# One VectorE subtraction per head, issued behind the projections' work instead of in front of it

## The chip, the cores and the metric

The kernel runs on one core of a Trainium2 chip. The metric is the device time of one launch in microseconds (us). Before the change three timed runs gave 684.11, 684.16 and 684.79 us; their median is 684.16 us.

## What is computed

One decoder layer over 528 tokens (16 meta tokens and 512 sequence tokens) of width 1024, in float32: sparse attention with 16 heads, then a SwiGLU feed-forward, each followed by a LayerNorm of `alpha * x + sublayer(x)`. A lightweight ReLU indexer scores every key for every query and keeps the 128 best; the attention of a head is then

```python
logits = q @ k.T * scale + bias[t5_bucket(distance)]      # -inf where not kept or not causal
p = softmax(logits)
out[head] = p @ v
h = layer_norm(alpha * h + concat(out) @ w_o)
h = layer_norm(alpha * h + (silu(h @ w_gate) * (h @ w_up)) @ w_down)
```

## The kernel before

**Products in two parts.** Every float32 operand of a matmul is held as a rounded high part and a low part, `lo = x - hi`, and a product is three matmuls: high by high, high by low, low by high (`mm3`, lines 283 to 289, matmuls at L286, L287, L288). ScalarE (ACT) makes the high part (`act_copy`), and VectorE (DVE) or GpSimd (POOL) the low part (`sub`, line 158, recorded as L159). Results of TensorE (PE) come from PSUM in the same two steps, so an evicted PSUM bank is read first by ACT and then by DVE.

**Weights.** They arrive in chunks of 128 x 1024. SyncE (SP) issues the load into one of three raw buffers (L188), ACT makes the high part, and for a chunk that is cut "late" the low part is not issued at once but put on the list `owed` (lines 199 to 201): columns 0 to 639 for DVE (`SHARE` = 640) and 640 to 1023 for POOL. `settle(engine)` issues what the list holds for that engine, `settle()` all of it (lines 205 to 209). `chunk(name)`, which every projection calls when it begins, also calls `settle()` (line 216). `stream()` (lines 610 to 618) cuts the next chunk of the queue `wq, wk, ..., wo` late and asks for the two loads behind it; the raw buffer of a load is free once ACT, DVE and POOL have read the chunk that was there. A chunk is cut about two projections ahead of the one that uses it.

**The loop over heads** (lines 871 to 928) is software-pipelined by hand; the order of the statements is the order of each engine's queue, since the schedule is manual. In its pass h the loop issues

1. on PE the scores of head h (`a{h}S`, L313 and L314) and the first two groups of transposes of head h-1's softmax (`turn(h-1, last, 0)` and `1`, L696);
2. on DVE the five logits instructions (L653), and on ACT the exponentials (`exps`, L661), of which the first two blocks go first; between them the meta part (`mh`, L687) and the two-part copies of the transposed tiles (`pt` and `ptl`, L156 on ACT and L159 on DVE);
3. `normalise(h, ..., (0, 1))`: a reciprocal on DVE (`rec`, L668) and two multiplications on POOL (`lg<-lg,rec`, L670);
4. `settle(nc.vector)` at line 900: the owed low part on DVE, 640 columns, when there is one;
5. the exponentials of the other two blocks, on ACT;
6. `fill(FILL[0])` at line 911: 2.3 units of the generator of projections (`pair`, lines 562 to 589). It gives one step of PE work at a time, and when the eight steps of a projection are through it evicts the PSUM bank: `queries` (q, ACT L156 and DVE L329) or `keys` (ka, ACT L156 and DVE L159), two instructions on each engine. Then it goes to the next projection, whose `chunk` call settles everything that is owed;
7. `turn(h-1, last, 2)` on PE, `normalise(h, ..., (2, 3))` with its own `rec`, `settle()` for POOL's share, and `part(h-1, 2, t2)`: the last two-part copy (`pt` of 256 columns) and `bd`, the block-diagonal meta part (L711), both on DVE;
8. `halved(2)` (the two parts of finished attention rows, `ath` on ACT and `atl` on DVE), `fill(FILL[1])`, and `values(h-1)`: eleven matmuls into `av` (L726), the last of which reads `bd`; ACT then copies half of it (`avt`) and DVE adds (`att`, L735);
9. `stream()`.

After the projections come the output projection, which starts inside the loop (`first_outputs`), LayerNorm, the feed-forward and the second LayerNorm.

PSUM has two banks for projections (`mm`), three for scores, two for transposes (`pt`) and one for `av`. A projection of the keys is done in two halves of 264 columns, each in a bank of its own.

Of the kernel before, what the change touches and what calls it, by code (L numbers as in the profile page):

```python
# [117 lines left out]
def trunk(ctx, tc, a, out):  # L118
    nc = tc.nc
# [38 lines left out]
    def sub(eng, o, x, y):  # L158
        eng.tensor_tensor(out=o, in0=x, in1=y.bitcast(F32), op=ALU.subtract)  # L159
# [45 lines left out]
    def settle(*engs):  # L205

        for x in [x for x in owed if not engs or x[0] in engs]:
            sub(*x)
            owed.remove(x)
# [99 lines left out]
    def scores(q2, ka, kb, name):  # L309
        banks = [bank(f"{name}S{i}", "S") for i in range(3)]  # L310
        for b, i, c, k0, n in REGIONS:
            o = banks[i][:, c : c + n]
            nc.tensor.matmul(o, q2[:, b * P : (b + 1) * P], ka[:, k0 : k0 + n], start=True, stop=False)  # L313
            nc.tensor.matmul(o, q2[:, b * P : (b + 1) * P], kb[:, k0 : k0 + n], start=False, stop=True)  # L314
        return banks
# [287 lines left out]
    def bias_load(h):  # L603
        if h < H:
            tzs[h] = sm.tile([P, 256], F32, name=f"tz{h}", tag="tz", bufs=2)
            nc.sync.dma_start(
                tzs[h], bass.AP(tensor=rbig.tensor, offset=rbig.offset + h * P * 384 + 127, ap=[[383, P], [1, 256]])
            )

    def stream(late=True):  # L610

        group, i = g_qk, where[using[0]][1]
        n = sum(c[0] in split for c in group)
        if n < min(i + 3, where["wo3"][1]):
            cut(group, n, late)
            n += 1
        load(group, n)
        load(group, n + 1)
# [21 lines left out]
    def bias(h, order=(1, 0, 3, 2)):  # L640
        if h < H:
            for b in order:
                n = min(W[b], 256)
                nc.gpsimd.tensor_tensor(  # L644
                    out=bm.at(b, W[b] - n, W[b]), in0=mask.at(b, W[b] - n, W[b]), in1=tzs[h][:, 256 - n :], op=ALU.add
                )

    def logits(h, banks, order):
        lg, mn = Logits(wide(f"lg{h}")), small(f"mn{h}", 5)
        for i in order:  # L650
            b, m, c, k0, n = REGIONS[i]
            init = mn[:, 1:2] if k0 else 3e38
            nc.vector.tensor_tensor_reduce(  # L653
                out=lg.at(b, k0, k0 + n), in0=banks[m][:, c : c + n], in1=bm.at(b, k0, k0 + n),
                scale=1.0, scalar=init, op0=ALU.add, op1=ALU.min, accum_out=mn[:, i : i + 1],
            )
        return lg, mn, small(f"den{h}", 4)

    def exps(lg, mn, den, n):
        b, i = ((1, 0), (0, 2), (3, 3), (2, 4))[n]  # L660
        nc.scalar.activation(  # L661
            lg.blk(b), lg.blk(b), AF.Exp, bias=mn[:, i : i + 1], scale=-1.0, accum_out=den[:, b : b + 1]
        )

    def normalise(h, lg, den, blocks=range(NB)):
        b0, b1 = min(blocks), max(blocks) + 1
        rec = small(f"rec{h}", 4)
        nc.vector.reciprocal(rec[:, b0:b1], den[:, b0:b1])  # L668
        for b in blocks:
            nc.gpsimd.tensor_tensor(  # L670
                out=lg.blk(b), in0=lg.blk(b), in1=rec[:, b : b + 1].to_broadcast([P, W[b]]), op=ALU.mult
            )
# [9 lines left out]
    def meta_parts(h, lg):  # L682

        x = metas[h] = sm.tile([P, P], F32R, name=f"mh{h}", tag="mh", bufs=1)
        xv = x.rearrange("p (r s t j) -> p r s t j", r=2, s=2, t=2)
        act_copy(xv[:, :, :, 0, :], lg.meta())
        nc.vector.tensor_tensor(  # L687
            out=xv[:, :, :, 1, :], in0=lg.meta(), in1=xv[:, :, :, 0, :].bitcast(F32), op=ALU.subtract
        )

    def turn(h, lg, n):

        pieces, cols = PLAN[n]
        pt = bank(f"pt{h}_{n}", "pt")
        for j, b, c in pieces:
            nc.tensor.transpose(pt[:, c : c + P], lg.at(b, NM + j * P, NM + (j + 1) * P), ident)  # L696
        if n == 2:
            nc.tensor.transpose(pt[:, cols : cols + P], metas[h].bitcast(F32), ident)
        return pt

    def part(h, n, pt):

        pieces, cols = PLAN[n]
        hi = unit(f"pt{h}_{n}", F32R)
        lo = hi[:, 256:] if cols == 256 else unit(f"ptl{h}_{n}", F32R)
        act_copy(hi[:, :cols], pt[:, :cols])
        sub(nc.vector, lo[:, :cols], pt[:, :cols], hi[:, :cols])
        parts[h, n] = (hi[:, :cols], lo[:, :cols])
        if n == 2:
            x = unit(f"bd{h}", F32R)[:, :S]  # L710
            nc.vector.tensor_tensor(  # L711
                out=x.rearrange("p (b q) -> p b q", q=P),
                in0=pt[:, cols : cols + P].rearrange("p (o q) -> p o q", o=1).to_broadcast([P, NB, P]),
                in1=diag.rearrange("p (b o) -> p b o", o=1).to_broadcast([P, NB, P]),
                op=ALU.mult,
            )
            parts[h, 3] = (x,)
# [55 lines left out]
    def halved(most=8):  # L773

        n = KT if paired else FEW
        for _ in range(most):
            if len(ath) < min(n, ready[0] // 2):
                halves()
# [61 lines left out]
    def broadcast(names, tiles):  # L840
        for n in names:
            for hf in range(2):
                t = tiles[n, hf] = unit(f"{n}_{hf}", tag="kq")[:, :512]
                nc.sync.dma_start(t, a[n][:, hf * 512 : hf * 512 + 512].to_broadcast([P, 512]))

    def x_load():
        for b in range(NB):
            y.append([unit(f"y{b}{hf}", tag="kq")[:, :512] for hf in range(2)])
            for hf in range(2):
                nc.sync.dma_start(y[b][hf], a["x"][b * P : (b + 1) * P, hf * 512 : hf * 512 + 512])  # L850
# [10 lines left out]
    def fill(us):  # L861
        due[0] += us
        while due[0] > 0:
            cost = next(rest, None)
            if cost is None:
                return
            due[0] -= cost
# [3 lines left out]
    for h in range(H + 1):  # L871
        while h < H and h not in KB:
            fill(0.1)
        if h < H:
            banks = scores(Q2[h], KA[h], KB[h], f"a{h}")
        if h == H:
            fill(FILL[2])
        if h:
            t0, t1 = turn(h - 1, last, 0), turn(h - 1, last, 1)
        if h < H:  # L880
            now = logits(h, banks, range(5) if h else (2, 0, 4, 1, 3))
            if h:
                bias(h + 1)
            if h == H - 1:
                free.append(True)
                broadcast(("g1", "b1"), gb1)
            bias_load(h + 2)
            if h == 0:
                fill(FILL0[0])
            exps(*now, 0)  # L890
        if h:
            meta_parts(h - 1, last)
            part(h - 1, 0, t0)
        if h < H:
            exps(*now, 1)
        if h:
            part(h - 1, 1, t1)
        if 0 < h < H:
            normalise(h, now[0], now[2], (0, 1))
        settle(nc.vector)  # L900
        if h < H:
            exps(*now, 2)
            exps(*now, 3)
        if h == 0:
            normalise(h, now[0], now[2])
            bias(1)
            stream()
            fill(FILL0[1])
            stream()
        else:  # L910
            fill((LATER if paired else FILL)[0])
        if h:
            t2 = turn(h - 1, last, 2)
        if 0 < h < H:
            normalise(h, now[0], now[2], (2, 3))
        settle()
        if h:
            part(h - 1, 2, t2)
            halved(2)
        fill((LATER if paired else FILL)[1])  # L920
        if h:
            values(h - 1)
            ready[0] = h
        stream()
        if h < H:
            last = now[0]
        if h == H - 2:
            x_load()
# [225 lines left out]
```

## Time and profile before

| | us |
|---|---|
| median of 3 timed runs | 684.16 |
| profiled execution, its own time | 686.96 |
| span of the profiled execution | 685.2 |
| passes 1 to 12 of the loop over heads, from the scores of head 1 to those of head 13 | 141 to 251 of the span |

| engine | busy us | share of the span |
|---|---|---|
| PE (matmuls) | 669.6 | 98% |
| DVE | 418.9 | 61% |
| ACT | 287.3 | 42% |
| POOL | 237.8 | 35% |

The granted TensorE clock of the profiled execution was 0.996. Times in a timeline are microseconds from the start of the span; the first column is the start, the second the length. `x2` means two instructions in a row, shown as one line. What stands in square brackets is how long the engine was idle before the line, and what ended that. Ends of matmuls are modelled, so the starts are what is compared.

### The profile page before, as it was taken

To read this page: it belongs to the slowest core of one execution; us is meant where nothing else is said; L and a number is where in the kernel's file an instruction comes from. 1 tells how busy PE (TensorE), PEld (TensorE's weight loads), DVE (VectorE), ACT (ScalarE), POOL (GpSimd) and SP (SyncE) were. 2 spreads that over 40 slices of the span, in tenths; PEclk is the share of its full clock that TensorE was granted. 3 is DMA by queue.
4 is the path that set the end of the run, shared out by engine and by line. 5 is a ranking of instruction groups with operands and counts; after the bars stand their busy time and mean duration, and the time that the engine had idled before them with its cause. 6 is when DMAs were issued, how large, how long until landed. Compare 5 with 4: busy or idle time off the path is not lost.

```text
span 685.2 us, 9428 instructions
## 1 busy us (share of the span) xinstructions
PE 669.6 (98%) x3440; PEld 565.6 (83%) x3440; DVE 418.9 (61%) x797; ACT 287.3 (42%) x516; POOL 237.8 (35%) x240
## 2 busy tenths in 40 slices
PE   8999999999999999999999999999999999999995
PEld 6888787889998888889888888888888888888884
DVE  5589897888888887696334243343433355575426
ACT  5473512567777775614323233232322334423310
POOL 2063812497786676653212121221212200011003
PEclk9999999999999999999999999999999999999998
DMA  6547130543133346410131322313132267745611
GB/s 235 173 148 258 58 75 17 152 152 85 56 103 87 93 114 211 154 62 31 63 122 63 123 80 105 114 70 123 61 123 83 102 224 233 244 152 193 195 51 61
DMA packets 31807, 83.11 MB, mean 121 GB/s; under 512 B 3745, under 2 KB 8913, under 8 KB 31761
## 3 DMA queue, kind: packets, MB, share of 16 engines
q1 hardware_dynamic: 31328, 82.12, 36.9%
q8 instruction: 27, 0.44, 0.3%
q10 hardware_dynamic: 432, 0.39, 0.2%
q14 instruction: 20, 0.16, 0.1%
HBM read 74.86 MB, written 5.27 MB: 117 GB/s over the span
## 4 chain that ended last, share of the span: by engine, by line
PE 51%; DVE 1%; POOL 0%; DVEq 0%; issue 0%
PE pd L1072 17%; PE p_wu L288 6%; PE p_wu L287 6%; PE p_wu L286 6%; PE p_wg L288 6%; PE p_wg L287 6%; PE p_wg L286 6%; DVE su L1082 0%; POOL fr L939 0%; DVE y L1081 0%; DVE y L956 0%; PE tz L971 0%; DVE mw L1087 0%; DVEq L1150 0%; DVE y L958 0%
## 5 line engine op out<-in xcount | busy, mean ns | idle before, releaser
L159 POOL TENSOR_TENSOR l_wu<-r_wu,h_wu 128x1024 fp32r<-128x1024 f32 x22 | 52.8, 2401 | 179.5 <-ACT h_wu L156 179.5
L1014 DVE TENSOR_TENSOR sg<-p_wu,sg 128x512 f32<-128x512 f32 x22 | 15.2, 692 | 107.8 <-PE p_wu L288 107.8
L159 DVE TENSOR_TENSOR l_wd<-r_wd,h_wd 128x1024 fp32r<-128x1024 f32 x36 | 45.4, 1263 | 41.9 <-ACT h_wd L156 41.7
L286 PE MATMUL p_wg<-h1h,h_wg 128*128 128x512 f32 (+1 forms) x184 | 70.0, 380 | 0.0
L286 PE MATMUL p_wu<-h1h,h_wu 128*128 128x512 f32 (+1 forms) x184 | 70.0, 380 | 0.0
L287 PE MATMUL p_wg<-h1l,h_wg 128*128 128x512 f32 (+1 forms) x184 | 69.9, 380 | 0.0
L288 PE MATMUL p_wu<-h1h,l_wu 128*128 128x512 f32 (+1 forms) x184 | 69.9, 380 | 0.0
L287 PE MATMUL p_wu<-h1l,h_wu 128*128 128x512 f32 (+1 forms) x184 | 69.9, 380 | 0.0
L288 PE MATMUL p_wg<-h1h,l_wg 128*128 128x512 f32 (+1 forms) x184 | 69.9, 380 | 0.0
L159 DVE TENSOR_TENSOR l_wg<-r_wg,h_wg 128x1024 fp32r<-128x1024 f32 x21 | 52.8, 2513 | 24.4 <-ACT h_wg L156 24.4
L156 ACT ACTIVATE hh<-sg 128x512 fp32r<-128x512 f32 x22 | 13.9, 632 | 119.3 <-DVE sg L1014 119.3
L670 POOL TENSOR_TENSOR lg<-lg,rec 128x144 f32<-128x144 f32 (+1 forms) x64 | 52.6, 846 | 21.9 <-DVE rec L668 21.1
L1072 PE MATMUL pd<-h_wd,hh 128*128 128x512 f32 (+1 forms) x162 | 59.6, 368 | 0.0
L1072 PE MATMUL pd<-h_wd,hl 128*128 128x512 f32 (+1 forms) x162 | 59.6, 368 | 0.0
L1072 PE MATMUL pd<-l_wd,hh 128*128 128x512 f32 (+1 forms) x162 | 59.5, 368 | 0.0
L156 ACT ACTIVATE h_wd<-r_wd 128x1024 fp32r<-128x1024 f32 x36 | 38.0, 1060 | 46.5 <-DMA r_wd<-in_wd 22.2
L644 POOL TENSOR_TENSOR bm<-score,tz 128x256 f32<-128x256 f32 (+1 forms) x64 | 43.9, 716 | 16.4 <-DVE mn L653 14.9
L939 POOL TENSOR_TENSOR fr<-fr,half_neg 128x1 f32<-128x1 f32 x4 | 4.0, 1004 | 117.5 <-DVE fr L938 117.0
L661 ACT ACTIVATE lg<-lg,mn 128x272 f32<-128x272 f32 (+1 forms) x64 | 36.3, 571 | 11.6 <-DVE mn L653 11.6
L287 PEld LDWEIGHTS p_wu<-h1l,h_wu 128*128 128x128 f32 x184 | 34.6, 188 | 6.6
L286 PEld LDWEIGHTS p_wg<-h1h,h_wg 128*128 128x128 f32 x184 | 34.6, 188 | 6.5
L286 PE MATMUL p_k<-hTh,h_wk 128*128 128x264 f32 x128 | 37.7, 295 | 2.3 <-DVE q L329 2.3
(337 smaller groups left out, 1753.0 us busy)
## 6 DMA issues: line engine op xcount, KB each, us to landing
r_wd<-in_wd SPq DMA_DIRECT2D x36, 512.0 KB, 4.3
r_wg<-in_wg SPq DMA_DIRECT2D x22, 512.0 KB, 3.7
r_wu<-in_wu SPq DMA_DIRECT2D x22, 512.0 KB, 4.5
kb<-ka SPq DMA_DIRECT2D x32, 132.0 KB, 2.3
r_wq<-in_wq SPq DMA_DIRECT2D x8, 512.0 KB, 4.8
r_wk<-in_wk SPq DMA_DIRECT2D x8, 512.0 KB, 3.4
rbig<-rdram SPq DMA_DIRECT2D x1, 3072.0 KB, 15.0
hTr<-in_hT SPq DMA_DIRECT2D x8, 264.0 KB, 5.3
```

Of the source, the lines that this page charges most:

```text
L156: nc.scalar.activation(o, i, AF.Copy, scale=scale)
L159: eng.tensor_tensor(out=o, in0=x, in1=y.bitcast(F32), op=ALU.subtract)
L286: nc.tensor.matmul(o, lh, rh, start=i == 0, stop=False)
L287: nc.tensor.matmul(o, lh, rl, start=False, stop=False)
L288: nc.tensor.matmul(o, ll, rh, start=False, stop=i == KT - 1)
L644: nc.gpsimd.tensor_tensor(out=bm.at(b, W[b] - n, W[b]), in0=mask.at(b, W[b] - n, W[b]), in1=tzs[h][:, 256 - n :], op=ALU.add)
L661: nc.scalar.activation(lg.blk(b), lg.blk(b), AF.Exp, bias=mn[:, i : i + 1], scale=-1.0, accum_out=den[:, b : b + 1])
L670: nc.gpsimd.tensor_tensor(out=lg.blk(b), in0=lg.blk(b), in1=rec[:, b : b + 1].to_broadcast([P, W[b]]), op=ALU.mult)
L939: nc.gpsimd.tensor_tensor(out=r, in0=r, in1=half_neg, op=ALU.pow)
L1014: nc.vector.tensor_tensor(out=sg, in0=pg[1], in1=sg, op=ALU.mult)
L1072: nc.tensor.matmul(pd[o], l[:, bs], r[:, c0:c1], start=f == 0 and i == 0, stop=f == NF - 1 and i == 2)
```

## The change

The call that issues DVE's owed low part moves from in front of the last two exponentials to behind the projections' work of that pass. Nothing is added or removed.

```diff
         if 0 < h < H:
             normalise(h, now[0], now[2], (0, 1))
-        settle(nc.vector)
         if h < H:
             exps(*now, 2)
             exps(*now, 3)
...
         else:
             fill((LATER if paired else FILL)[0])
+        settle(nc.vector)
         if h:
             t2 = turn(h - 1, last, 2)
         if 0 < h < H:
```

## Rows read from the trace of the kernel before

**Rows 1.** The page: busy time of each engine.

```profile
PE 669.6 (98%) x3440; PEld 565.6 (83%) x3440; DVE 418.9 (61%) x797; ACT 287.3 (42%) x516; POOL 237.8 (35%) x240
```

**Rows 2.** Waits of PE: who waited for whom, us in total, times, longest.

```profile
PE p_k L286 <- DVE q L329: 2.3, 2, 1.3
...
PE pt L696 <- DVE ptl L159: 1.1, 4, 0.4
```

**Rows 3.** Timeline, pass 3, ACT and DVE around the eviction (start, length, engine, line).

```profile
163.73 0.80 DVE L159 TENSOR_TENSOR l_wk<-r_wk,h_wk 128x640 fp32r<-128x640 f32 x1
...
164.06 0.79 ACT L156 ACTIVATE ka<-p_k 64x264 fp32r<-64x264 f32 x2
...
164.87 0.89 DVE L159 TENSOR_TENSOR ka<-p_k,ka 64x264 fp32r<-64x264 f32 x2 [0.34 <-ACT ka L156]
...
166.34 0.68 DVE L711 TENSOR_TENSOR bd<-pt,diag 128x512 fp32r<-128x512 f32 x1
```

**Rows 4.** Timeline, pass 4, DVE: the same place with an eviction of q.

```profile
172.53 0.80 DVE L159 TENSOR_TENSOR l_wq<-r_wq,h_wq 128x640 fp32r<-128x640 f32 x1
...
174.08 1.39 DVE L329 SCALAR_TENSOR_TENSOR q<-p_q,q 64x512 fp32r<-64x512 f32 x2 [0.75 <-ACT q L156]
...
176.03 0.68 DVE L711 TENSOR_TENSOR bd<-pt,diag 128x512 fp32r<-128x512 f32 x1
```

**Rows 5.** Timeline, pass 5, DVE: no eviction between the low part and bd.

```profile
182.37 0.80 DVE L159 TENSOR_TENSOR l_wk<-r_wk,h_wk 128x640 fp32r<-128x640 f32 x1
...
183.48 0.68 DVE L711 TENSOR_TENSOR bd<-pt,diag 128x512 fp32r<-128x512 f32 x1
```

**Rows 6.** Timeline, PE: the matmul of values that reads bd, six passes.

```profile
167.07 0.50 PE L726 MATMUL av<-bd,vm 128*128 128x512 f32 x1
...
176.76 0.50 PE L726 MATMUL av<-bd,vm 128*128 128x512 f32 x1 [0.21 <-DVE bd L711]
...
203.45 0.49 PE L726 MATMUL av<-bd,vm 128*128 128x512 f32 x1
...
222.73 0.39 PE L726 MATMUL av<-bd,vm 128*128 128x512 f32 x1
...
232.20 0.50 PE L726 MATMUL av<-bd,vm 128*128 128x512 f32 x1
...
250.89 0.39 PE L726 MATMUL av<-bd,vm 128*128 128x512 f32 x1
```

**Rows 7.** Timeline, DVE: bd in passes 7, 9, 10 and 12.

```profile
202.71 0.68 DVE L711 TENSOR_TENSOR bd<-pt,diag 128x512 fp32r<-128x512 f32 x1
...
221.44 0.68 DVE L711 TENSOR_TENSOR bd<-pt,diag 128x512 fp32r<-128x512 f32 x1
...
231.47 0.68 DVE L711 TENSOR_TENSOR bd<-pt,diag 128x512 fp32r<-128x512 f32 x1
...
249.28 0.68 DVE L711 TENSOR_TENSOR bd<-pt,diag 128x512 fp32r<-128x512 f32 x1
```

**Rows 8.** Timeline, POOL: pass 3 with a low part on DVE, pass 8 without one.

```profile
163.98 1.43 POOL L670 TENSOR_TENSOR lg<-lg,rec 128x144 f32<-128x144 f32 x2 [0.82 <-DVE rec L668]
...
165.38 1.02 POOL L159 TENSOR_TENSOR l_wk<-r_wk,h_wk 128x384 fp32r<-128x384 f32 x1
...
209.14 1.03 POOL L670 TENSOR_TENSOR lg<-lg,rec 128x144 f32<-128x144 f32 x2 [0.82 <-DVE rec L668]
```

**Rows 9.** Timeline, passes 1, 3, 9 and 10: low parts beside POOL's work, and PE's wait.

```profile
146.24 1.27 DVE L159 TENSOR_TENSOR l_wq<-r_wq,h_wq 128x640 fp32r<-128x640 f32 x1
...
166.94 0.82 DVE L159 TENSOR_TENSOR atl<-att,ath 128x512 fp32r<-128x512 f32 x1
...
222.04 1.60 DVE L159 TENSOR_TENSOR atl<-att,ath 128x512 fp32r<-128x512 f32 x1
...
228.31 0.44 PE L696 MATMUL pt<-ident,lg 128*128 128x128 f32 x2 [0.45 <-DVE ptl L159]
```

**Rows 10.** Timeline, pass 4, SP: the load behind the low part.

```profile
175.22 0.33 SPq L188 DMA_DIRECT2D r_wk<-in_wk  x1
```

## The prediction

> **What bounds the kernel now.** I read the page first: PE is busy for 98% of the span, every other engine for 61% or less [rows 1]. So time is lost or won only where PE waits, and a piece of work on DVE matters through the instructions behind it in DVE's queue that PE needs. Next the waits of PE: the whole list is a few microseconds, and in the loop over heads three kinds stand in it. PE waits for DVE's eviction of q before it may write the next half of the keys into that bank (2.3 us in two places, the longest 1.3), for `ptl`, whose end frees a transpose bank (1.1 us in four) [rows 2], and for `bd`, which the last matmul of `values` reads [rows 6]. Last I read the timeline of each pass, DVE beside PE, to see who is in front of whom.
>
> What the moved instruction stands next to decides all. In a pass that has an owed low part DVE's queue is: `rec` of the first two blocks, the low part, the evictions of `fill` (if one falls there), `rec` of the other two blocks, `pt`, `bd`. The change puts the low part behind the evictions, which is at the same time directly in front of the second `rec`, `pt` and `bd`.
>
> **Where the order changes at all.** Only where an eviction falls into the first `fill` of a pass that has something owed. By the timeline of DVE these are six passes: 3, 7, 10 and 12 with keys, 4 and 9 with q. Passes 3 and 4 stand in the rows [rows 3, 4], the other four look like them. In passes 1 and 5 nothing of the projections lies between, as pass 5 shows [rows 5], passes 2 and 8 owe nothing, pass 0 settles at the same place in the queue, and from pass 13 on the output projection's `chunk` settles before any work. A `chunk` call can't empty the list ahead of the eviction in these six: 2.3 units of `fill` are fewer than the eight steps (2.64 or 5.2 units) from the start of a projection to its eviction. The call that follows the eviction issues the low part, so it lands right behind the eviction.
>
> **What it gives.** The evictions could start earlier by up to the low part's 0.80 us, if it held them up. It doesn't: in pass 3 DVE is idle for 0.34 us between the low part and the eviction, until ACT's two copies, 164.06 to 164.85, are both over; DVE starts at 164.87 [rows 3]. In pass 4 the idle time is 0.75 us [rows 4], in the other four 0.34 to 0.76. So the gain is zero, and DVE idles 0.80 us more there. The bank is not freed sooner, and the 1.3 us wait for q stays.
>
> **What it costs: the step behind the evictions.** Now `bd` ends 1.26 us after the eviction of pass 3 ends (164.87 + 0.89 = 165.76 to 166.34 + 0.68 = 167.02) [rows 3], and 1.24 us in pass 4 (175.47 to 176.71) [rows 4]. With the low part directly in front of `rec`, `pt` and `bd`, as pass 5 has it now, it is 183.48 + 0.68 - 182.37 = 1.79 us from the low part's start [rows 5]. The difference is 0.53 to 0.55 us, less than 0.80, since without a wait between them DVE's instructions overlap a little; I take 0.54.
>
> Who waits for that: the matmul that reads `bd`. It starts 0.05 us after `bd` ends in pass 3 (167.07 against 167.02) [rows 3, 6] and in pass 4 (176.76 against 176.71) [rows 4, 6], 0.06 in pass 7 (203.45 against 203.39) and 0.05 in pass 10 (232.20 against 232.15) [rows 6, 7]: PE arrives there with `bd` already the last thing it needs, so the delay shows in full. In pass 9 it starts 0.61 us after `bd` (222.73 against 222.12) and in pass 12 0.93 us after (250.89 against 249.96) [rows 6, 7]: covered. Sum: 4 x 0.54 = 2.16 us.
>
> **POOL beside it.** While the low part runs, POOL's two multiplications of pass 3 take 1.43 us; in pass 8, with no low part, 1.03 [rows 8]. So the two engines hinder each other. Moved, the low part lets POOL's multiplications go 0.40 us faster, which nothing waits for, and POOL's own share of the chunk starts at 163.98 + 1.03 = 165.01 and ends at 166.03. DVE's low part, ready at 165.76, meets it. If it waits it out, that is 0.27 us more in pass 3, and as much in pass 7, which has the same sequence: 0.54 us. If not, nothing. A low part that runs beside POOL has taken 1.27 us instead of 0.80 [rows 9], so I take the 0.54. In passes 4 and 10 POOL's share is over, or stands behind.
>
> The Trainium skill ("SBUF — State Buffer", section "Who interferes with whom") says that a VectorE instruction with two SBUF inputs and a GpSimd one that reads SBUF exclude each other for a whole instruction, and the one that starts second waits. The trace agrees in kind: 0.40 us lost by POOL here. By that rule the sum is 2.7 us, without it 2.2.
>
> **Pass 9 and what follows.** `bd` is covered, but DVE's queue then runs without a pause up to the `ptl` for which PE waits 0.45 us at 228.31 [rows 9]; a delay of 0.54 would show there in full. Against it stands that `atl` took 1.60 us there beside POOL's multiplications, where it took 0.82 in pass 3 [rows 9]. Those multiplications follow the delayed `rec`, `atl` meets another moment of them, and may win 0.8 us back: between +0.54 and -0.25. I take 0.
>
> **Other queues.** SP: the load into the raw buffer of this chunk waits for all its readers. In pass 4 it goes out at 175.22 [rows 10]; DVE's low part would end at 175.47 + 0.80 = 176.27, so the load, and the bias load behind it, go 1.05 us later, more than one pass (some 9 us) before they are used. The moved step issues no DMA itself. POOL's second pair of multiplications follows the delayed `rec`, but the transposes that read it come after PE's own delay. The low part is used two projections later. All three: zero.
>
> **Sum.** 2.16 + 0.54 + 0 = 2.7 us slower. The profiled execution took 686.96 us, 2.80 above the median of the timed runs, 684.16; the difference goes on either: 689.7 there, **686.9 us** as a median. Bounds: 2.16 - 0.25 = 1.9 (686.1) without POOL's term and with the gain of pass 9; and, with the low part at 1.27 instead of 0.80 in all four, 4 x (0.54 + 0.47) + 0.54 = 4.6 (688.8).
>
> **Rivals.**
> 1. *Faster: the bank comes free sooner.* Place: the eviction of q in pass 9, for which PE waits 1.3 us [rows 2]. If the low part held up that eviction, the whole wait could go: 684.16 - 1.3 = 682.9. It decides from the point where DVE ends the low part after ACT ends its copies. Against it: ACT ends last by 0.34 to 0.76 us in all six [rows 3, 4]. [...] Chance 0.06.
> 2. *No difference: the order doesn't change, or the delay is covered.* If `chunk` settles ahead of the evictions, the queues are the same: 684.2. If the matmuls' records are late by a few tenths, so that PE has cover I don't see, half or less of 2.16 is left: up to 685.3. Against it: the count of steps above, and starts that follow `bd` by the same 0.05 us three times. Chance 0.16.
> 3. *Worse: POOL's term is large.* Every moved low part runs at 1.27 us and pass 9 pays too: 688.8. For it: 1.27 in pass 1 [rows 9]. Against it: POOL waits for the second `rec` in most of these places, and DVE's low part then runs alone. Chance 0.10.
>
> **How the numbers follow.** The forecast has 0.68, the rivals 0.06, 0.16 and 0.10. A measurement of this kernel tells about 0.2%, 1.4 us, from no change. The forecast and rival 3 lie beyond it: slower 0.78. Rival 2 is within: same 0.16. Rival 1, at 1.3 us, would be at the edge; I leave its chance to faster: 0.06. The range reaches down into rival 2, to 684.8, and up to 688.8; it leaves out rival 1 and most of rival 2.
>
> **What would show it.** Right: in passes 3, 4, 7 and 10 DVE's low part begins right after the eviction, the idle time in front of the eviction grows by 0.8 us, and `av<-bd` starts about 0.5 to 0.8 us later against the matmul in front of it; PE's waits on `bd` sum to over 2 us, those on q stay at 2.3. Wrong: if the evictions start earlier against the matmuls in front, if PE's wait on q shrinks, or if `bd` keeps its distance to the eviction.

## The result: slower, and by more than forecast

The change took 690.76 us as the median of 4 runs (689.5 to 691.1), before 684.47 us beside it: ratio 1.0085, 95% interval 1.0066 to 1.0104. Timed again beside before it was 1.0060 (1.0046 to 1.0073), 4.1 us. The forecast was slower, 686.9 us in a range up to 688.8: the direction was right, the size was not.

| | before | after |
|---|---|---|
| profiled execution, own time, us | 686.96 | 690.51 |
| span, us | 685.2 | 688.7 |
| PE busy, us | 669.6 | 670.9 |
| `av<-bd` of pass 2 to that of pass 13, us | 100.64 | 104.86 |

The page of the changed kernel, busy time of each engine, the line that answers to [rows 1]:

```profile
PE 670.9 (97%) x3440; PEld 565.7 (82%) x3440; DVE 420.8 (61%) x797; ACT 287.3 (42%) x516; POOL 234.5 (34%) x240
```

No engine has more work to speak of. What PE waits for has changed, by the list of its waits in the changed kernel (us in total, times, longest), which answers to [rows 2]:

```profile
PE p_k L286 <- DVE q L329: 2.3, 2, 1.3
...
PE pt L696 <- DVE ptl L159: 1.5, 4, 0.9
PE av L726 <- DVE pt L159: 1.5, 4, 0.8
...
PE av L726 <- DVE bd L711: 0.9, 4, 0.2
```

The wait for q is where it was. The wait of `av` for `pt` is new, and that for `bd`, 0.2 us in one place before [rows 6], is now 0.9 in four. Of DVE's timeline these are passes 3 and 4, beside [rows 3] and [rows 4]:

```profile
164.23 0.89 DVE L159 TENSOR_TENSOR ka<-p_k,ka 64x264 fp32r<-64x264 f32 x2 [1.07 <-ACT ka L156]
165.15 0.85 DVE L159 TENSOR_TENSOR l_wk<-r_wk,h_wk 128x640 fp32r<-128x640 f32 x1
165.93 0.15 DVE L668 RECIPROCAL rec<-den 128x2 f32<-128x2 f32 x1
166.12 0.42 DVE L159 TENSOR_TENSOR pt<-pt,pt 128x256 fp32r<-128x256 f32 x1
166.46 0.68 DVE L711 TENSOR_TENSOR bd<-pt,diag 128x512 fp32r<-128x512 f32 x1
167.06 1.61 DVE L159 TENSOR_TENSOR atl<-att,ath 128x512 fp32r<-128x512 f32 x1
...
174.42 1.39 DVE L329 SCALAR_TENSOR_TENSOR q<-p_q,q 64x512 fp32r<-64x512 f32 x2 [1.48 <-ACT q L156]
175.84 0.83 DVE L159 TENSOR_TENSOR l_wq<-r_wq,h_wq 128x640 fp32r<-128x640 f32 x1
176.59 0.16 DVE L668 RECIPROCAL rec<-den 128x2 f32<-128x2 f32 x1
...
177.12 0.68 DVE L711 TENSOR_TENSOR bd<-pt,diag 128x512 fp32r<-128x512 f32 x1
```

DVE idles 1.07 us in front of the eviction where it idled 0.34, and 1.48 where it idled 0.75: 0.73 us more in both. The low part was taken out of time in which DVE waited for ACT anyway, and now stands in front of `rec`, `pt` and `bd`. From the end of the eviction of pass 3 (165.12) to the end of `bd` (167.14) it is now 2.02 us, not 1.26. And `atl`, behind `bd`, takes 1.61 us, not the 0.82 of [rows 9].

PE's matmuls that read `bd`, passes 2, 3, 4, 7, 9, 10 and 12, answer to [rows 6]; the transposes at 231.12 answer to those at 228.31 in [rows 9]:

```profile
157.60 0.39 PE L726 MATMUL av<-bd,vm 128*128 128x512 f32 x1
...
167.19 0.50 PE L726 MATMUL av<-bd,vm 128*128 128x512 f32 x1 [0.22 <-DVE bd L711]
...
177.85 0.50 PE L726 MATMUL av<-bd,vm 128*128 128x512 f32 x1 [0.21 <-DVE bd L711]
...
205.30 0.50 PE L726 MATMUL av<-bd,vm 128*128 128x512 f32 x1 [0.21 <-DVE bd L711]
...
224.98 0.50 PE L726 MATMUL av<-bd,vm 128*128 128x512 f32 x1
...
231.12 0.44 PE L696 MATMUL pt<-ident,lg 128*128 128x128 f32 x2 [0.90 <-DVE ptl L159]
...
235.74 0.50 PE L726 MATMUL av<-bd,vm 128*128 128x512 f32 x1 [0.21 <-DVE bd L711]
...
254.46 0.41 PE L726 MATMUL av<-bd,vm 128*128 128x512 f32 x1
```

Taken from one `av<-bd` to the next, the time lost in each pass can be read off; a start that is earlier or later as a whole drops out. The forecast's terms stand beside it.

| pass | before, us | after, us | lost | forecast |
|---|---|---|---|---|
| 3 | 8.82 | 9.59 | 0.77 | 0.81 |
| 4 | 9.69 | 10.66 | 0.97 | 0.54 |
| 7 | 8.85 | 9.65 | 0.80 | 0.81 |
| 8 | 8.80 | 9.02 | 0.22 | 0 |
| 9 | 10.48 | 10.66 | 0.18 | 0 |
| 10 | 9.47 | 10.76 | 1.29 | 0.54 |
| 5, 6, 11, 12, 13 together | 44.53 | 44.52 | -0.01 | 0 |
| pass 2 to pass 13 | 100.64 | 104.86 | 4.22 | 2.70 |

Behind pass 13 both traces run alike to within 0.1 us.

### The profile page after: what moved, and what is told of

Same layout as the page of the kernel before. It is cut to its first block, busy times and chain, and to the rows that moved or that the text cites. A ratio compares the mean times of both kernels' runs of the same rounds, so it can differ in the third digit from the quotient of the medians.

```text
span 688.7 us, 9429 instructions
## 1 busy us (share of the span) xinstructions
PE 670.9 (97%) x3440; PEld 565.7 (82%) x3440; DVE 420.8 (61%) x797; ACT 287.3 (42%) x516; POOL 234.5 (34%) x240
## 4 chain that ended last, share of the span: by engine, by line
PE 51%; DVE 1%; POOL 0%; DVEq 0%; issue 0%
PE pd L1072 17%; PE p_wu L286 6%; PE p_wu L287 6%; PE p_wu L288 6%; PE p_wg L286 6%; PE p_wg L287 6%; PE p_wg L288 6%; DVE su L1082 0%; POOL fr L939 0%; DVE y L1081 0%; DVE y L956 0%; PE tz L971 0%; DVE mw L1087 0%; DVE y L958 0%; DVEq L1150 0%
## 5 line engine op out<-in xcount | busy, mean ns | idle before, releaser
L670 POOL TENSOR_TENSOR lg<-lg,rec 128x144 f32<-128x144 f32 (+1 forms) x64 | 49.2, 794 | 28.0 <-DVE rec L668 25.5
L288 PEld LDWEIGHTS p_wu<-h1h,l_wu 128*128 128x128 f32 x184 | 34.6, 188 | 6.6
L288 PEld LDWEIGHTS p_wg<-h1h,l_wg 128*128 128x128 f32 x184 | 34.6, 188 | 6.6
```

Of the source, the lines that this page charges most:

```text
L288: nc.tensor.matmul(o, ll, rh, start=False, stop=i == KT - 1)
L670: nc.gpsimd.tensor_tensor(out=lg.blk(b), in0=lg.blk(b), in1=rec[:, b : b + 1].to_broadcast([P, W[b]]), op=ALU.mult)
```

## Experiments

The column that the traces give is the length from the `av<-bd` of pass 2 to that of pass 13; the ratio is timed against runs of before on the same chip.

| run | edit | pass 2 to 13, us | ratio to before (95%) |
|---|---|---|---|
| e0_same | before, unchanged | 100.60 | 1.0009 (1.0000 to 1.0018) |
| e1_after | the change again | 104.89 | 1.0060 (1.0046 to 1.0073) |
| e2_behind_bd | low part behind `bd` | 105.92 | 1.0080 (1.0065 to 1.0094) |
| e3_pass3_only | moved in pass 3 alone | 101.57 | 1.0020 (1.0009 to 1.0032) |
| e4_after_atl | the change, `atl` put off | 103.31 | 1.0035 (1.0023 to 1.0048) |
| e5_before_atl | before, `atl` put off | 100.49 | 1.0001 (0.9991 to 1.0012) |
| e6_before_reversed | before, evictions reversed | 99.20 | 0.9973 (0.9959 to 0.9987) |
| e7_both | before, both of these | 99.86 | 0.9990 (0.9979 to 1.0001) |
| e8_after_reversed | the change, evictions reversed | 102.68 | 1.0021 (1.0008 to 1.0035) |
| e9_reversed_again | as e6 | 99.16 | 0.9984 (0.9973 to 0.9996) |

### Before and the change once more (e0_same, e1_after)

No edit to either kernel.

> The kernel before, unchanged, to see how much its own executions differ and what a second trace of it looks like. If the first profiled execution of before (686.96 us, 2.80 above its median) was an exceptional one, this trace has the last scores, a15S, earlier against the first ones than there, and a span some 2 to 3 us under 685.2. If the 2.80 us are what profiling adds in every execution, the span comes out at 685 again. The ratio to before is 1.000 within its interval by every theory.

> The change again, with five rounds on one chip beside before. By the two traces the six passes cost 4.2 us (the start differed by 0.6 us the other way): ratio 1.006. If something outside the loop over heads also costs, as the first timing says (1.0085), the ratio is 1.008 or more, and 1.5 us or more are lost outside passes 3 to 10.

The loop repeats to 0.04 us in before and to 0.03 us in the change, and the 4.3 us between them agree with the timed 4.1 us. What differs between executions lies in front of pass 2's `av<-bd`: the first scores of the indexer start at 24.80 us of the span in the first trace of before, at 23.38 in the second, and anywhere from 21.8 to 24.9 over all traces of this study, and from there to `av<-bd` of pass 2 it is 133.3 to 133.8 us, with the change and without. The second span of before was 684.0, 1.2 us under the first. So nothing outside the loop is lost by the change as far as two traces of each show. The 1.0085 of the first timing is about 1.6 us more than the traces bear out; its interval and that of the second timing overlap (1.0066 to 1.0073), and a variation of this size is found between executions of one kernel. More than that isn't settled. The kernel before, timed against itself, came out at 1.0009, so a difference of 0.001 in the table says nothing by itself; the lengths in the loop are the finer measure.

### One pass alone (e3_pass3_only)

The edit against the kernel before:

```diff
-        settle(nc.vector)
+        if h != 3:
+            settle(nc.vector)
...
             fill((LATER if paired else FILL)[0])
+        settle(nc.vector)
```

> The low part is moved in pass 3 alone. Theory: PE loses 0.75 us at the av matmuls of pass 3, and another 0.2 us in pass 4, because atl in pass 3 takes 1.6 instead of 0.8 us beside POOL and DVE reaches pass 4 late: 0.9 to 1.0 us in all, ratio 1.0014. Rival (each moved low part costs on its own, pass 4 costs more because it evicts q): 0.75 us, with pass 4 as in before (PE's wait on bd 0.5 us there).

The loop is 0.97 us longer than in the second trace of before. Pass 3 lost 0.76 us, and pass 4, in which nothing was moved, 0.21 (the matmuls of passes 3 and 4, on PE's timeline; 9.90 us apart, 9.69 before):

```profile
167.17 0.50 PE L726 MATMUL av<-bd,vm 128*128 128x512 f32 x1 [0.21 <-DVE bd L711]
...
177.07 0.50 PE L726 MATMUL av<-bd,vm 128*128 128x512 f32 x1 [0.21 <-DVE bd L711]
```

So one moved low part costs in two passes. The rival, a dearer pass 4, falls: in the change pass 4 loses 0.97 us, and less the 0.21 that come from pass 3 this is 0.76, the same as pass 3.

### Behind bd (e2_behind_bd)

```diff
-        settle(nc.vector)
+        if 0 < h < 13:
+            kept_back.append(True)
+        else:
+            settle(nc.vector)
...
         if h:
             part(h - 1, 2, t2)
+            kept_back.clear()
+            settle()
             halved(2)
```

While `kept_back` holds, `chunk()` and the `settle()` behind normalise issue POOL's share alone; DVE's stands behind `bd`. This holds for passes 1 and 5 too, where the change itself alters nothing.

> The low part stands behind the evictions and also behind bd, in every pass 1 to 12 that owes one. Theory (what costs is that the low part stands in front of the second rec, pt and bd): PE's waits on pt and bd in passes 3, 4, 7 and 10 are back at before's 0.1 to 0.5 us each, not 0.8 to 1.5, and the time is within 1 us of before; 0.2 to 0.5 us may be lost where DVE reaches the logits of the next pass later. Rival (what costs is that the low part is late, whoever stands behind it, through raw buffers or POOL): the time stays at that of the change, 4 us or more above before.

Half of it came as expected. Passes 3, 7 and 9 lose nothing at `bd`, and PE's waits on `pt` and `bd` are nearly gone, but the wait on `ptl`, at the third group of transposes of the next pass, has risen to 5.2 us, and the kernel is slower than the change. Of its 5.3 us over before, 0.45 stand in pass 6, behind the low part of pass 5, which the change leaves alone. First the list of PE's waits, then POOL and DVE in pass 3:

```profile
PE pt L696 <- DVE ptl L159: 5.2, 8, 1.2
...
PE av L726 <- DVE pt L159: 0.2, 1, 0.2
PE av L726 <- DVE bd L711: 0.2, 1, 0.2
```

```profile
166.33 1.88 POOL L670 TENSOR_TENSOR lg<-lg,rec 128x400 f32<-128x400 f32 x2
...
167.16 1.73 DVE L159 TENSOR_TENSOR l_wk<-r_wk,h_wk 128x640 fp32r<-128x640 f32 x1
168.81 0.68 DVE L159 TENSOR_TENSOR atl<-att,ath 128x512 fp32r<-128x512 f32 x1
```

The low part starts while POOL multiplies, ends 0.7 us after POOL's second multiplication (168.21), and takes 1.73 us instead of 0.80. `att`, the logits and `ptl` of the next pass stand behind it without a pause. The expectation held the wait at `bd` right and missed this. Both halves say the same of DVE: behind the evictions there is no idle time left to put 0.8 us into, neither in front of `bd` nor behind it.

The Trainium skill ("SBUF — State Buffer", section "Who interferes with whom") has the rule for it: such a pair of instructions excludes each other, and the one that starts first keeps the other out. The trace agrees, here with 0.93 us lost by DVE.

### atl put off (e4_after_atl, e5_before_atl)

```diff
         act_copy(hi, att[p][:, :S])
-        sub(nc.vector, lo, att[p][:, :S], hi)
+        late_low.append((nc.vector, lo, att[p][:, :S], hi))
...
             normalise(h, now[0], now[2], (0, 1))
+        low_halves()
```

`low_halves()` issues what `late_low` holds, in the next pass, behind the first reciprocals and POOL's multiplications that read them; in before it stands behind the low part. From pass 13 on `atl` stays where it was.

> The change, and in passes 3, 5, 7 and 9 the low half of the finished attention rows (atl) is put off into the next pass, behind its first rec, where DVE idles over 1 us in the changed kernel. Theory: what the change costs beyond the four waits at pt and bd is atl, which meets POOL's multiplications after the delayed rec and makes DVE late in the next pass. So the steps at bd of pass 3 (0.77), 7 (0.81) and 10 (0.7) stay, that of pass 4 falls from 0.93 to 0.75, those at the transposes of pass 8 (0.20) and 10 (0.44) go, and PE's waits on ptl in passes 6 and 10, which before has too (0.3 and 0.6 us), go as well: 1.5 to 2 us under the change, about 2.5 above before. Rival (the later steps are DVE's second share of the low part alone): within 0.5 us of the change.

> The kernel before with atl put off in the same way, behind the low part. By the theory DVE has 0.34 to 0.76 us idle in front of the evictions of passes 4 and 10 and more in 6 and 8; atl takes 0.7 to 1.6 us. PE's waits on ptl in passes 6 (0.34 us) and 10 (0.6 us) go, and up to 0.8 us may come up in pass 4, where the eviction of q is pushed back: between 0.9 us faster and no change. If atl has no part in it: no change.

On top of the change, the loop gets 1.6 us shorter, and pass by pass it is the expected list: pass 3 still loses 0.78 us against before and pass 7 0.82, pass 4 now 0.75, pass 8 0.07. The timed difference, 1.0060 to 1.0035, is 1.7 us. So the 0.2 us of passes 4 and 8, and the loss at the transposes of pass 10, came through `atl`: `rec` and `atl` both come later, and `atl` now starts just after the second multiplication of POOL's second pair has begun. In the changed kernel this pair runs from 166.23 in pass 3, its second instruction from 167.04:

```profile
163.32 1.03 POOL L670 TENSOR_TENSOR lg<-lg,rec 128x144 f32<-128x144 f32 x2 [0.82 <-DVE rec L668]
164.31 1.02 POOL L159 TENSOR_TENSOR l_wk<-r_wk,h_wk 128x384 fp32r<-128x384 f32 x1
166.23 1.88 POOL L670 TENSOR_TENSOR lg<-lg,rec 128x400 f32<-128x400 f32 x2 [0.90 <-DVE rec L668]
...
167.04 1.07 POOL L670 TENSOR_TENSOR lg<-lg,rec 128x528 f32<-128x528 f32 x1
```

The same second instruction in before:

```profile
167.17 1.52 POOL L670 TENSOR_TENSOR lg<-lg,rec 128x528 f32<-128x528 f32 x1
```

In before `atl` started 0.23 us ahead of it (166.94, [rows 9]) and took 0.82 us, and POOL's instruction was the one that took longer, 1.52 us. In the change `atl` started 0.02 us behind it (167.06) and took 1.61.

POOL's first pair is back at 1.03 us, as forecast from [rows 8], and nothing gains by it.

In before, putting `atl` off does nothing in the sum (1.0001): pass 10 gains 0.6 us at its transposes and pays 0.4 back at `bd`, where `atl` now stands in front of the eviction. Behind the low part DVE idled 0.75 us in pass 4 and 0.36 in pass 10; `atl` took 0.91 in each.

### The evictions reversed (e6_before_reversed, e8_after_reversed, e7_both, e9_reversed_again)

```diff
-        for x, ka in zip(rows, heads):
+        for x, ka in reversed(list(zip(rows, heads))):
             sub(nc.vector, ka[64:128, t0:t1], x, ka[0:64, t0:t1])
...
-        for x, q in zip(rows, q2):
+        for x, q in reversed(list(zip(rows, q2))):
             if scale == 1.0:
```

DVE now evicts the half in partitions 64 to 127 first.

> The kernel before with DVE's two eviction instructions in the other order: the one that reads PSUM partitions 64 to 127 first, 0 to 63 second. Theory (an instruction on DVE overlaps the one in front of it only if its PSUM input starts at the same partition as the last PSUM read; so pt starts 0.20 us after rec behind an eviction and 0.07 us without one): in passes 3, 4, 7, 8 and 10 pt starts 0.07 to 0.10 us after rec, bd ends 0.1 us earlier, and PE's waits on bd shrink by 0.1 us each: 0.5 us faster, ratio 0.9993. Rival (the 0.20 us come from the wait on ACT's pt or from rec itself): pt stays 0.20 us behind rec, no change.

DVE's `rec` and `pt` in pass 3 of before:

```profile
165.80 0.17 DVE L668 RECIPROCAL rec<-den 128x2 f32<-128x2 f32 x1
166.00 0.42 DVE L159 TENSOR_TENSOR pt<-pt,pt 128x256 fp32r<-128x256 f32 x1
```

And DVE's timeline of pass 3 in before with reversed evictions:

```profile
162.12 0.88 DVE L159 TENSOR_TENSOR ka<-p_k,ka 64x264 fp32r<-64x264 f32 x2 [0.34 <-ACT ka L156]
163.03 0.17 DVE L668 RECIPROCAL rec<-den 128x2 f32<-128x2 f32 x1
163.11 0.40 DVE L159 TENSOR_TENSOR pt<-pt,pt 128x256 fp32r<-128x256 f32 x1
163.43 0.68 DVE L711 TENSOR_TENSOR bd<-pt,diag 128x512 fp32r<-128x512 f32 x1
```

`pt` starts 0.08 us after `rec`, where it was 0.20 behind an eviction, and `bd` ends 1.11 us after the eviction instead of 1.26. The rivals (ACT's `pt`, or `rec` itself) are out, since neither was touched. From one `av<-bd` to the next the loop gains 0.13 us in pass 3, 0.14 in pass 4, 0.01 in pass 7, 0.24 in pass 8, 0.76 in pass 10 and 0.12 in pass 11, 1.4 us in all. The tenth at `bd` was expected; that half of the gain is in pass 10, 0.6 us of it at the transposes, was not. There `atl` of pass 9 took 0.71 us, in before 1.60.

The Trainium skill ("VectorE: DVE Perf Modes", section "Two Vector instructions with no wait between them") gives the rule, as a model: an instruction whose PSUM input starts in another group of 32 partitions than the last PSUM read waits until all earlier ones have ended. The trace agrees: behind an eviction that ends on partitions 64 to 127 `pt` starts 0.03 us after `rec` has ended, otherwise 0.09 us before; the difference is 0.12 us.

> The change together with DVE's reversed evictions. Theory (a low part put in front of rec, pt and bd costs from its own start to the start of rec, 0.75 us, whether pt overlaps rec or not; the 0.54 of the prediction came from comparing a pass with that overlap with one without): pt comes 0.07 to 0.10 us behind rec, the steps at bd of passes 3 and 7 against the kernel before with reversed evictions are 0.75 us again, and the whole is 0.4 to 0.6 us faster than the change: ratio 1.005. If the overlap itself makes the low part cheaper, the steps are 0.54 us.

With the change on top, pass 3 of DVE reads:

```profile
164.31 0.87 DVE L159 TENSOR_TENSOR l_wk<-r_wk,h_wk 128x640 fp32r<-128x640 f32 x1
165.10 0.15 DVE L668 RECIPROCAL rec<-den 128x2 f32<-128x2 f32 x1
165.17 0.40 DVE L159 TENSOR_TENSOR pt<-pt,pt 128x256 fp32r<-128x256 f32 x1
...
166.09 0.70 DVE L159 TENSOR_TENSOR atl<-att,ath 128x512 fp32r<-128x512 f32 x1
```

Against e6 pass 3 loses 9.44 - 8.69 = 0.75 us, the same as without the reversal, and pass 7 0.67: there PE in e6 came 0.19 us after `bd` and had some cover. So the low part costs from its own start to that of `rec`, 0.8 us less the little that `rec` overlaps, in either order. The whole came out better than expected, 1.0021 instead of 1.005: with `rec`, `pt` and `bd` 0.13 us earlier, `atl` is in time (0.70 us in passes 3 and 7, 0.71 in 9), and passes 4 and 7 to 10 lose less. A tenth of a microsecond decides there.

> The kernel before with both: atl put off and the evictions reversed. If both theories hold, the gains add: 0.5 to 1.4 us faster than before, ratio 0.998 to 0.9993. If only one holds, this equals that one.

> The kernel before with reversed evictions once more, on another call's runs, since it came out ahead of before: 0.9973 again if the gain is real (the trace of the first showed 1.5 us in the loop over heads, so 0.998 would bear it out too); 1.000 if it was the start of the program, which was 1.6 us shorter there than in the second trace of before.

The two don't add: e7 is 0.7 us behind e6 in the loop, 0.39 of it in pass 10, where the deferred `atl` again stands in front of the eviction. The reversal alone repeats (99.16 us, ratio 0.9984), so with reversed evictions the kernel is ahead of before by 0.16 to 0.27%, and of the change by more.

## Why the prediction was right in its direction and short in its size

**Where the order changes, and the gain of zero: right.** The evictions of six passes changed places with the low part and no others; DVE's new idle time ends with ACT's copies in each, and PE's wait for q is 2.3 us before and after. The rival that the bank comes free sooner is out. So is the rival of no difference.

**The price of the moved step, 0.54 us: wrong, 0.75.** This is the first step that failed. It compared the stretch behind an eviction in pass 3, in which `pt` waits out `rec` (0.20 us), with pass 5, in which `pt` overlaps it (0.07 us). The overlap belongs to the pass, not to the low part. Like for like, from the low part's start to that of `rec` in pass 5, it would have been 183.09 - 182.37 = 0.72, from these rows of before's DVE timeline beside [rows 5]:

```profile
183.09 0.15 DVE L668 RECIPROCAL rec<-den 128x2 f32<-128x2 f32 x1
183.16 0.40 DVE L159 TENSOR_TENSOR pt<-pt,pt 128x256 fp32r<-128x256 f32 x1
```

In pass 3 the runs show 0.75 to 0.77 with either order of the evictions (e3, e8). The sign that the forecast named, PE's waits on `bd` over 2 us, came only with those on `pt` of the same stretch: 0.9 and 1.5.

**POOL's term, 0.27 us in passes 3 and 7: wrong.** The low part took 0.85 us in pass 3 and 0.90 in pass 7:

```profile
203.21 0.90 DVE L159 TENSOR_TENSOR l_wk<-r_wk,h_wk 128x640 fp32r<-128x640 f32 x1
```

In passes 4, 9 and 10, with POOL idle, it took 0.83 behind the eviction, so the collision with POOL's share of the chunk cost 0.02 and 0.07. The two errors cancel in passes 3 and 7 (0.81 forecast, 0.77 and 0.80 measured) and don't in 4 and 10. In pass 3 POOL's share ended at 165.33, 0.18 us after the low part had started, so most of the overlap that the forecast priced at 0.27 us was there. The forecast had assumed that DVE waits it out, and DVE did not; the exclusion that e2 shows in full shows hardly at all here, and why stays open.

**Pass 9 covered, and nothing behind it: wrong.** With 0.54 us `bd` of pass 9 was just covered by 0.56; with 0.75 it isn't: 0.18 us there. The forecast named the way into pass 10 (DVE without a pause up to `ptl`) and both ends, +0.54 and -0.25, and took 0 between them. `atl` did not win, it took 1.60 us again, and PE's wait at the transposes of pass 10 went from 0.45 to 0.90 us. From `av<-bd` of pass 9 to these transposes 0.56 us are lost.

**atl in passes 3 and 7: not in the sum.** The forecast looked at `atl` only in pass 9. In passes 3 and 7 it went from 0.82 and 0.86 to 1.61 and 1.60 us, DVE came late to passes 4 and 8, and 0.2 us were lost in each (e3 and e4).

**The other queues: right.** In the changed kernel SP's load of pass 4 goes out at 176.82, 1.6 us later than in before, of which 0.3 is the shift of the trace (the eviction of q starts at 174.42 instead of 174.08); nobody waits for it. POOL's second pair waits longer for `rec` and its readers come later still.

**The range.** Its upper end, 4.6 us, lies above the 4.2 us of the traces by luck: it stood on low parts of 1.27 us in all four passes, as rival 3 did, and none there took more than 0.90.

Added up: four low parts at 0.73 to 0.80 are 3.1 us, `bd` of pass 9 and what follows it into pass 10 0.7, and `atl` in passes 4 and 8 0.4: the 4.2 us of the traces. By its ratio the first timing showed 5.8 us, the second 4.1; what the first had beyond the traces stays open.

## What to carry to other kernels

An engine that idles in front of an instruction is a place to put work for nothing, as far as the idle time reaches (`atl` of 0.91 us in 0.36 us of it was too much); before work is moved out of such a place, look at what it will stand in front of then, and whether anybody waits for that at once. What an inserted instruction costs is read from its own start to the start of the next one, and two stretches are compared only if they overlap alike. Where two engines exclude each other, a delay of a few tenths also changes who meets whom: follow it into the next pass.

## What the runs showed of the hardware

The order of two independent DVE instructions decided over 0.12 us of the second instruction behind them: 0.20 us from `rec` to `pt` where the last PSUM read in front had started at partition 64, 0.08 where it had started at partition 0. Seven such places (passes 3, 4, 7 to 10 and 12), and what followed from them, made 1.4 us of 100.6 in the loop.

DVE's subtraction of 640 columns with both inputs in SBUF took 0.80 us where it started ahead of POOL's instruction, 0.83 behind an eviction with POOL idle, 0.85 to 0.90 where it met the end of a POOL instruction, and 1.73 where POOL's multiplication of 528 columns had just begun (e2). `atl`, 512 columns, took 0.82 us where it started 0.23 us ahead of that multiplication and 1.61 where it started 0.02 us behind it.
